# Banded attention: value products on quarters of the array, two shared PSUM banks, and one written order for all engines

## The chip, the cores and the metric

The kernel runs on one core of one Trainium2 chip. The core has five engines with queues of their own: TensorE (PE in the profile; its weight loads are the row PEld), VectorE (DVE), ScalarE (ACT), GpSimd (POOL) and SyncE (SP, which here only issues DMAs). The metric is the device time of one execution in microseconds (us).

## The reference

One step of a two-layer encoder over a prompt of 2048 tokens and a sample of 32 tokens, 1024 channels. The first layer is a gated delta rule, the second a sliding-window attention with learned sinks. Only the second is touched. For a query chunk of 64 tokens it reads the keys and values of its own chunk and of the two before it, so at most 192 keys:

```python
def sink_softmax(s, sinks):
    sk = sinks.astype(jnp.float32)[..., None, None]
    m = jnp.maximum(s.max(-1, keepdims=True), sk)
    p = jnp.exp(s - m)
    return p / (p.sum(-1, keepdims=True) + jnp.exp(sk - m))

def swa_layer(x, k, v, pos, cached, w_in, sinks, w_out, ln_g, ln_b):
    proj = x @ w_in
    q = rope_partial(proj[..., :B_QW].reshape(b, l, B_Q_HEADS, B_HD), pos) * (B_HD ** -0.5)
    z = proj[..., B_QW:]
    o = cached_attention(q, k, v, sk) if cached else banded_attention(q, k, v, sk)
    out = (o * jax.nn.silu(z)) @ w_out
    return layer_norm(DN_ALPHA * x + out, ln_g, ln_b)
```

There are 16 query heads of 64 channels in four groups, one key and value head to a group. The prompt uses the banded form, the sample (32 tokens) a cached window of 128 keys and its own 32. All is float32.

## The kernel before

Up to the attention the kernel projects the input, runs the delta rule and its output layer, and then projects keys, values, queries and the gate z of the second layer in blocks of 416 tokens, in weight slabs of 128 columns (`project`, L74: three f32r products for each of 8 k, high by high, high by low and low by high part). Queries, gates, keys and values go to scratch in HBM (`bq`, `bz`, `bk`, `bv`). The last gate blocks, tokens 0 to 831 of slabs 4 to 7, are computed beside the first chunks; therefore the chunks go in the order 14 to 31, then 0 to 13.

`Attention.chunk(n)` handles 64 queries. It has two passes p, each over two key-value heads (`half` 0 and 1) of four query heads. In a pass:
- scores: four float32 products, each with 64 channels as rows; `half` 0 uses rows 0 to 63, `half` 1 rows 64 to 127 (L1596, out `S`). In the profile a float32 product stands as two passes.
- `softmax` (L1465): largest score (L1470) and minimum with the sink (L1471) on DVE, four exponentials with row sums on ACT (L1478), the sink's exponential (L1479, L1480), sum and reciprocal on DVE (L1481, L1482); then POOL multiplies the probabilities by it (L1604, twice).
- six transposes on PE into two `tr` banks (L1611), copied to `pt` by ACT (L1613) and DVE (L1615).
- values: `vd` holds, for each chunk of 64 keys, a 128 by 128 matrix with the two heads' values on its diagonal and zeros off it. One product for each of up to three key chunks adds up in `ot` (L1617). DVE multiplies by the gate into `graw` (L1620).

After every second chunk a tile of 128 tokens is complete and queued in `pend`. `finish` (L1485) makes its output: high and low part of the gated rows (ACT L1491, POOL L1492), then for each half c of the 1024 output columns 24 products of 512 columns (L1124 to L1126, out `po`), the addition to the residual (L1132), statistics (L1504), a reciprocal root in three Newton steps (L490 to L494), the normalisation on ACT (L1513) and two passes over 1024 columns on POOL (L1514, L1515).

PSUM has eight banks: two scores tiles of two banks, two for transposes, one for values and one for output products. The order of instructions in this stage is not written: a scheduler places them by a modelled timeline. It has PE run products wherever a chunk waits. `flush` keeps two or three finished tiles in reserve for that, and the rest is made after the last chunk, in the scores' banks (`late`).

Of the kernel before, what the change touches and what calls it, by code (L numbers as in the profile page):

```python
# [1069 lines left out]
def load_kept_weights(nc, pool, kept):  # L1070

    w = pool.tile([128, 2, KC, D], F32R, tag="wo", name="wo")
    yield w[:, 0], w[:, 1]
    for k in range(KC):
        nc.sync.dma_start(w[:, :, k].bitcast(F32), kept[:, k].rearrange("a p d -> p a d"))
        yield


# [38 lines left out]
def out_products(nc, ps, ghi, glo, w, k, cs, n):  # L1117

    a, z = k == 0, k == KC - 1
    if n <= 64:  # L1120
        nc.tensor.matmul(ps[:2 * n], ghi[:, k, :2 * n], w[0][:, k, cs], start=a, stop=z, skip_group_check=True)
        nc.tensor.matmul(ps[:n], ghi[:, k, :n], w[1][:, k, cs], start=False, stop=z, skip_group_check=True)
        return
    nc.tensor.matmul(ps[:n], ghi[:, k, :n], w[0][:, k, cs], start=a, stop=False)  # L1124
    nc.tensor.matmul(ps[:n], ghi[:, k, :n], w[1][:, k, cs], start=False, stop=False)  # L1125
    nc.tensor.matmul(ps[:n], glo[:, k, :n], w[0][:, k, cs], start=False, stop=z)  # L1126
# [12 lines left out]
class OutNorm:  # L1139
# [30 lines left out]
    def tile(self, parts, r, n, tail=False):  # L1170
# [5 lines left out]
        for c in range(2):  # L1176
            cs = slice(c * 512, c * 512 + 512)
            ps = self.pp.tile([128, 512], F32, tag="po", name="po")
            for k in range(KC):
                out_products(nc, ps, ghi, glo, w, k, cs, n)  # L1180
                if k % 2 == 1:
                    yield (4 if n <= 64 else 6) * 0.227
# [228 lines left out]
class Attention:  # L1411


    def __init__(self, tc, left, I, O, T, G):
# [4 lines left out]
        self.two = new_pool(tc, left, "t_two", 2, side=L)  # L1419
        self.thr = new_pool(tc, left, "t_thr", 3, side=L)  # L1420
# [6 lines left out]
        self.vd = one.tile([128, 32, 2, 128], F32, tag="vd", name="vd")  # L1427
# [10 lines left out]

    def open_right(self, right):
# [4 lines left out]
        self.pp = new_pool(tc, right, "u_pp", 1, PSUM, side=R)  # L1444
        self.ps_s.append(new_pool(tc, right, "u_ps", 1, PSUM, side=R))
        self.rest = load_kept_weights(self.nc, self.oone, self.T["wob"])
        self.w = next(self.rest)
        next(self.rest)
        self.tabs = ln_tables(self.nc.sync, self.oone, I["b_ln_g"], I["b_ln_b"])

    def load_kv(self, a, z):
        nc, T = self.nc, self.T
        nc.sync.dma_start(self.kT[:, :, a * 64:z * 64], T["bk"][:, :, a * 64:z * 64].rearrange("a p t -> p a t"))
        src = T["bv"][0:NP, :].rearrange("(c k) (p d) -> k c p d", k=64, p=2)
        for i in range(2):
            rows, off = slice(i * 64, i * 64 + 64), slice(64 - i * 64, 128 - i * 64)
            nc.gpsimd.memset(self.vd[rows, a:z, :, off], 0.0)
            for p in range(2):
                nc.sync.dma_start(self.vd[rows, a:z, p, rows], src[:, a:z, p, rows])
# [4 lines left out]

    def softmax(self, S, P, nskc):  # L1465

        nc, V, thr = self.nc, self.nc.vector, self.thr
        nsub = len(P)
        nm = thr.tile([128, 4], F32, tag="nm", name="nm")
        V.tensor_reduce(out=nm[:, :nsub], in_=S, axis=AX.X, op=ALU.max, negate=True)  # L1470
        V.tensor_tensor(out=nm[:, :nsub], in0=nm[:, :nsub], in1=nskc, op=ALU.min)  # L1471
        sm = thr.tile([128, 4], F32, tag="sm", name="sm")
        es_ = thr.tile([128, 4], F32, tag="es", name="es")
        for u in range(nsub):
            src = S[:, u, :]
            if len(P[u].shape) == 3:
                src = src.rearrange("r (j k) -> r j k", k=64)
# [104 lines left out]
    def chunk(self, n):  # L1582
# [38 lines left out]
        if n % 2 == 1:  # L1621
            self.pend.append(((n - 1) * 64, 128, graw))
# [284 lines left out]
```

## Time and profile before

| | us |
|---|---|
| median of 3 runs | 2173.01 (2172.12 to 2175.58) |
| the profiled execution | 2172.59 |
| its span, first to last instruction | 2170.7 |
| PE busy | 2136.9 (98%) |
| DVE, ACT, POOL busy | 1369.1, 898.9, 837.7 |
| first scores pass of the attention (L1596) | 1749.6 |

The attention stage is what comes after about 1730 us. Busy time of PE counts overlapping passes once. Where a line of a timeline has a count (x6), the row merges so many instructions of one kind: its duration is from the first start to the last end. In summaries of one line, three numbers are the shortest, median and longest duration in ns. "[... <-X]" is idle time before an instruction and what ended it.

### The profile page before, as it was taken

The numbers are of one execution on the slowest core, as the hardware profiler recorded it, in microseconds if no ns is written. First come the engines' busy times: TensorE is split into PE (matmuls) and PEld (weight loads), VectorE is DVE, ScalarE is ACT, GpSimd is POOL, SyncE is SP. The second block draws the span as 40 slices with busy tenths as digits, with TensorE's granted clock in tenths as the row PEclk, the third lists the DMA queues.
The fourth block names the chain that finished last, engine by engine and source line by source line (L and its number), as shares of the span: only waits on it lengthen the run. The fifth ranks groups of instructions, "written<-read, shape, count | busy, mean of one in ns | idle before, by whom it ended". The sixth has DMA issues, their size and how long they took to land.

```text
span 2170.7 us, 36895 instructions
## 1 busy us (share of the span) xinstructions
PE 2136.9 (98%) x13690; PEld 1973.4 (91%) x13690; DVE 1369.1 (63%) x2718; ACT 898.9 (41%) x2273; POOL 837.7 (39%) x1185
## 2 busy tenths in 40 slices
PE   8999999999999999999999999999999999999998
PEld 6999999999999999999988888999999987778885
DVE  3676666765648688779868875035442236668775
ACT  4444444356522466667742213221112235444442
POOL 1422222212132377767811102155441215546564
PEclk9999999999999999999999999999999999999999
DMA  5213323257575544447747755364211287233321
GB/s 200 69 60 100 108 91 110 72 163 223 152 229 154 170 162 157 149 161 231 257 146 230 225 174 154 101 233 154 75 69 67 87 193 256 79 98 97 107 64 53
DMA packets 268116, 308.28 MB, mean 142 GB/s; under 512 B 79729, under 2 KB 198833, under 8 KB 267665
## 3 DMA queue, kind: packets, MB, share of 16 engines
q1 hardware_dynamic: 256688, 282.45, 41.7%
q10 hardware_dynamic: 11248, 23.48, 3.3%
q8 instruction: 108, 1.77, 0.3%
q14 instruction: 72, 0.58, 0.1%
HBM read 189.63 MB, written 116.60 MB: 141 GB/s over the span
## 4 chain that ended last, share of the span: by engine, by line
PE 93%; DVE 3%; DMA 2%; ACT 1%; issue 0%; POOL 0%; ACTq 0%; DVEq 0%; POOLq 0%
PE ps L78 17%; PE ps L80 17%; PE ps L79 17%; PE po L1124 5%; PE po L1126 5%; PE po L1125 5%; PE ot L1617 4%; PE S L1596 2%; PE tr L1611 2%; PE g L674 1%; PE ks L816 1%; PE gq L801 1%; PE sp L816 1%; PE op L840 1%; PE vp L816 1%; PE op L846 1%
## 5 line engine op out<-in xcount | busy, mean ns | idle before, releaser
L78 PE MATMUL ps<-act_hi,w_hi 128*128 128x416 f32 x2000 | 706.4, 354 | 3.0 <-ACT w_hi L54 2.3
L80 PE MATMUL ps<-act_hi,w_lo 128*128 128x416 f32 x2000 | 705.0, 353 | 1.3 <-POOL w_lo L55 1.1
L79 PE MATMUL ps<-act_lo,w_hi 128*128 128x416 f32 x2000 | 701.2, 351 | 0.4 <-DVE act_lo L70 0.4
L78 PEld LDWEIGHTS ps<-act_hi,w_hi 128*128 128x128 f32 x2000 | 376.8, 189 | 8.8 <-ACT w_hi L54 3.1
L80 PEld LDWEIGHTS ps<-act_hi,w_lo 128*128 128x128 f32 x2000 | 375.9, 188 | 6.3 <-POOL w_lo L55 1.6
L79 PEld LDWEIGHTS ps<-act_lo,w_hi 128*128 128x128 f32 x2000 | 376.1, 188 | 5.0 <-DVE act_lo L70 0.8
L55 POOL TENSOR_TENSOR w_lo<-w_raw,w_hi 128x1024 fp32r<-128x1024 f32 x44 | 117.0, 2658 | 474.0 <-ACT w_hi L54 437.7
L208 DVE SCALAR_TENSOR_TENSOR y<-R,convw,y 128x2083 f32<-128x2083 f32 x72 | 182.7, 2538 | 62.5 <-ACT y L205 46.8
L1604 POOL TENSOR_TENSOR P<-P,sm 128x384 f32<-128x384 f32 (+2 forms) x128 | 100.5, 807 | 172.0 <-DVE sm L1482 103.6
L708 POOL TENSOR_TENSOR tm<-L,Tt 128x60 f32<-128x60 f32 (+19 forms) x365 | 124.6, 341 | 97.8 <-issue 39.6
L710 POOL TENSOR_TENSOR Tt<-Tt,tm 128x60 f32<-128x60 f32 (+19 forms) x365 | 143.6, 393 | 28.6
L1478 ACT ACTIVATE P<-S,nm 128x192 f32<-128x192 f32 (+3 forms) x260 | 104.8, 419 | 90.2 <-DVE nm L1471 43.6
L304 ACT COPY R<-ps 128x416 f32<-128x416 f32 (+1 forms) x144 | 60.3, 442 | 107.7 <-PE ps L80 96.0
L1124 PE MATMUL po<-wo_hi,g_hi 128*128 128x512 f32 x256 | 103.3, 404 | 0.0
L1322 POOL TENSOR_TENSOR rs<-rs,sin 128x416 f32<-128x416 f32 x50 | 70.7, 1414 | 79.3 <-DVE rs L1321 73.5
L1126 PE MATMUL po<-wo_hi,g_lo 128*128 128x512 f32 x256 | 100.2, 391 | 0.6 <-DVE g_lo L1167 0.6
L1125 PE MATMUL po<-wo_lo,g_hi 128*128 128x512 f32 x256 | 99.9, 390 | 0.0
L1617 PE MATMUL ot<-pt,vd 128*128 128x256 f32 x372 | 97.1, 387 | 1.6 <-ACT pt L1613 1.1
L1407 DVE SCALAR_TENSOR_TENSOR za<-zs,za 128x416 f32<-128x416 f32 x40 | 32.2, 808 | 96.6 <-ACT za L1406 96.5
L1124 PE MATMUL po<-wo,g_hi 128*128 128x512 f32 x224 | 92.9, 415 | 0.0
L54 ACT CAST w_hi<-w_raw 128x1024 fp32r<-128x1024 f32 x48 | 50.4, 1050 | 101.9 <-PE ps L79 74.6
L1126 PE MATMUL po<-wo,g_lo 128*128 128x512 f32 x224 | 90.1, 402 | 0.0
(304 smaller groups left out, 4072.9 us busy)
## 6 DMA issues: line engine op xcount, KB each, us to landing
w_raw<-in_w_in SPq DMA_DIRECT2D x40, 512.0 KB
w_raw<-in_b_w_in SPq DMA_DIRECT2D x20, 512.0 KB
k<-s_k SPq DMA_DIRECT2D x17, 512.0 KB
E<-s_E SPq DMA_DIRECT2D x17, 512.0 KB
s_bz<-za SPq DMA_DIRECT2D x40, 208.0 KB
s_bq<-ra SPq DMA_DIRECT2D x40, 208.0 KB
s_q<-y SPq DMA_DIRECT2D x8, 1024.0 KB
s_wo<-wo_parts SPq DMA_DIRECT2D x16, 512.0 KB
```

The source lines that it names most:

```text
L55: sub.tensor_tensor(out=lo[:], in0=raw[:], in1=hi[:], op=ALU.subtract)
L78: nc.tensor.matmul(ps, hi[:, k, :], xh[:, k, :], start=(k == 0), stop=False)
L79: nc.tensor.matmul(ps, hi[:, k, :], xl[:, k, :], start=False, stop=False)
L80: nc.tensor.matmul(ps, lo[:, k, :], xh[:, k, :], start=False, stop=(k == KC - 1))
L208: nc.vector.scalar_tensor_tensor(out=y[:], in0=R[:, j:j + W], scalar=self.convw[:, i, j:j + 1], in1=y[:], op0=ALU.mult, op1=ALU.add)
L708: P.tensor_tensor(out=tm[:n, i0 - k:, :w], in0=L[:n, i0:, j:j + 1].to_broadcast(sh), in1=Tt[:n, j:j + 1, :w].to_broadcast(sh), op=ALU.mult)
L710: P.tensor_tensor(out=Tt[:n, i0:, :w], in0=Tt[:n, i0:, :w], in1=tm[:n, i0 - k:, :w], op=ALU.subtract)
L1124: nc.tensor.matmul(ps[:n], ghi[:, k, :n], w[0][:, k, cs], start=a, stop=False)
L1125: nc.tensor.matmul(ps[:n], ghi[:, k, :n], w[1][:, k, cs], start=False, stop=False)
L1126: nc.tensor.matmul(ps[:n], glo[:, k, :n], w[0][:, k, cs], start=False, stop=z)
L1478: nc.scalar.activation(P[u], src, AF.Exp, bias=nm[:, u:u + 1], scale=1.0, accum_out=sm[:, u:u + 1])
L1617: nc.tensor.matmul(ot[:, p], self.vd[:, kc0 + j, p, :], pt[:, 2 * j:2 * j + 2, :], start=(j == 0), stop=(j == nj - 1))
```

## The change

Three things change together, all in the second layer's attention.

Values: `vd` is now 64 columns wide and has no zeros. For each key chunk there are four products of 64 rows by 64 columns (p and `half`), each on its own quarter of the array. The rows are the keys of one half, the output partitions p * 64 to p * 64 + 63; the two halves go to two banks. The order of heads in the gate's weight slabs, and that of the rows of the output weights, is changed on the host to match.

Banks: the output products of column half c use the same bank as the values of `half` c (`out_bank`). The bank that held them alone is gone; the scores' banks no longer hold output products.

Order: `chunk`, `softmax` and `finish` are cut into small steps, and `run` writes them out in one order for all five engines, with scores two chunks ahead of the values, transposes one chunk ahead, and the output products of one tile spread over two chunks. `step` places single steps of the previous tile's normalisation between other DVE operations. The gate pieces (12 products each) are placed among the first chunks with `fill`. Slabs 6 and 7, still loaded, go first, so that only slabs 4 and 5 are loaded again. Two of the eight k slices of the output weights are loaded early, into room on the left.

```diff
-        self.vd = one.tile([128, 32, 2, 128], F32, tag="vd", name="vd")
+        self.vd = one.tile([128, 32, 2, 64], F32, tag="vd", name="vd")
...
-            nc.gpsimd.memset(self.vd[rows, a:z, :, off], 0.0)
...
+    def out_bank(self, i):
+        return self.ps_o.tile([128, 512], F32, tag=("oa", "ob")[i], name="ot")
...
+    def product(self, x, c, part):
+        cs = slice(c * 512, c * 512 + 512)
+        if part == 0:
+            x.ps = self.out_bank(c)
+        for k in range(part * KC // 2, (part + 1) * KC // 2):
+            out_products(self.nc, x.ps, x.ghi, x.glo, (self.w[k][:, 0, cs], self.w[k][:, 1, cs]), k, x.n)
...
+    def norm(self, x):
+        nc, V, pool, n = self.nc, self.nc.vector, self.otwo, x.n
+        x.mv = pool.tile([128, 2], F32, tag="mv", name="mv")
+        V.bn_aggr(out=x.mv[:n], in_=x.st[:n])
+        yield
...
+        yield from newton_steps(nc, pool, ve, x.rs, n, 1, "ln")
...
+    def affine(self, x):
+        n, tabs = x.n, self.tabs
+        self.nc.gpsimd.tensor_tensor(out=x.r[:n], in0=x.r[:n], in1=tabs[0][:n], op=ALU.mult)
+        self.nc.gpsimd.tensor_tensor(out=x.r[:n], in0=x.r[:n], in1=tabs[1][:n], op=ALU.add)
...
+    def values(self, n, pts):
+        nc = self.nc
+        kc0, nj = self.keys(n)
+        banks = [self.out_bank(half) for half in range(2)]
+        for j in range(nj):
+            for p in range(2):
+                for half in range(2):
+                    hs, ps = slice(half * 64, half * 64 + 64), slice(p * 64, p * 64 + 64)
+                    nc.tensor.matmul(banks[half][ps, :256], self.vd[hs, kc0 + j, p, :], pts[p][hs, 2 * j:2 * j + 2, :],
+                                     start=(j == 0), stop=(j == nj - 1))
+        return banks
...
+        def largest(i, p, between=iter(())):
+            if i <= last:
+                x = soft[i, p]
+                self.largest(x)
+                step(1)
+                next(between, None)
+                self.with_sink(x)
+
+        def exps(i, p):
+            if i <= last:
+                x = soft[i, p]
+                self.exps(x)
+                step(1)
+                self.sink_exp(x)
+
+        def shares(i, p):
+            if i <= last:
+                x = soft.pop((i, p))
+                self.total(x)
+                step(1)
+                self.inverse(x)
+                self.shares(x)
...
+        fill(3)
+        early(0, 0)
+        fill(2)
+        shares(0, 0)
+        early(0, 1)
+        fill(2)
+        shares(0, 1)
+        early(1, 0)
+        turn(0, 0)
+        copies(0, 0)
+        fill(2)
+        turn(0, 1)
+        copies(0, 1)
+        shares(1, 0)
+        score(1, 1)
+        fill(1)
+        po = following = stored = None
+        for i in range(last):
+            c = i % 2
+            if c == 0:
+                if i >= 4:
+                    done, po = po, following
+                if i + 4 < last and i != 2:
+                    self.start(order[i + 4])
...
+            banks = self.values(order[i], got(i))
+            gated = self.gated(order[i], banks, c)
+            lean = i < 4
+            largest(i + 1, 1, iter(()) if lean else gated)
+            exps(i + 1, 1)
+            drain(gated)
+            if i < 2:
+                fill(1)
+            score(i + 2, 0)
+            turn(i + 1, 0)
+            if lean:
+                largest(i + 2, 0)
+                shares(i + 1, 1)
+                copies(i + 1, 0)
+                exps(i + 2, 0)
+            else:
+                copies(i + 1, 0)
+                largest(i + 2, 0)
+                exps(i + 2, 0)
+            if i < 2:
+                fill(2)
+            if po:
+                self.product(po, c, 0)
+            if i >= 5:
+                x = po if c else done
+                if x:
+                    self.stats(x, 1 - c)
+                    if c == 0:
+                        norm[:] = x, self.norm(x)
+            step(2)
+            if not lean:
+                shares(i + 1, 1)
+            step(4)
+            shares(i + 2, 0)
+            if c == 0 and i >= 2:
+                following = self.finish(*self.pend.pop(0))
+                self.cast(following)
+                self.rest(following)
+            if c == 1 and norm[0]:
+                step(20)
+                self.normed(norm[0])
+                self.affine(norm[0])
+                stored, norm[0] = norm[0], None
+            if c == 0 and stored:
+                self.store(stored)
+                stored = None
+            if po:
+                self.product(po, c, 1)
+                self.added(po, c)
+            turn(i + 1, 1)
+            copies(i + 1, 1)
+            if i == 1:
+                self.start(order[6])
+                opened()
+            score(i + 2, 1)
...
-    for n in order:
-        for _ in range(2):
-            next(att.rest, None)
-        att.chunk(n)
...
+    with tc.manual_schedule(engines={ET.PE, ET.DVE, ET.Activation, ET.Pool, ET.SP}):
+        att.load_keys(12, 18)
+        att.start(14)
+        att.load_values(12, 18)
+        att.start(16)
+        att.run(gates(), opened)
```

Here `cast` and `rest` are the high and low part (ACT, POOL), `normed` is the normalisation on ACT, `added` and `stats` the addition to the residual and the statistics, and `turn`/`turned` the transposes. After the loop `run` makes the tiles that are left (the last two and the sampled one) with the same steps, and the last one ends in `tail` on DVE as before.

More of the change, by code (lines that the diff above doesn't have):

```diff
@@ L2 @@
 import math
+import types
 from contextlib import ExitStack
@@ L1485, in finish, with open_softmax @@
[L1485 to L1494 removed]
+    def open_softmax(self, S, P, nskc, whole):
+        x = types.SimpleNamespace(S=S, P=P, nskc=nskc, whole=whole, n=len(P))
+        x.nm, x.sm, x.es = (self.thr.tile([128, 4], F32, tag=t, name=t)[:, :x.n] for t in ("nm", "sm", "es"))
+        return x
```

470 lines of the change are left out of this document (292 added, 178 removed).

## The prediction

> **What bounds the kernel now.** I read the page first, for the span and for the engine that fills it.
>
> ```profile
> span 2170.7 us, 36895 instructions
> PE 2136.9 (98%) x13690; PEld 1973.4 (91%) x13690; DVE 1369.1 (63%) x2718; ACT 898.9 (41%) x2273; POOL 837.7 (39%) x1185
> ```
>
> The change touches only the attention stage, the last 440 us, so I asked next for a window of its steady part (columns: window, its length, busy time of PE, PEld, DVE, ACT, POOL, granted clock, DMA share, GB/s), and then for the chain of waits there.
>
> ```profile
> 2004.40:2094.00 89.60, 89.60 (x514) 73.19 (x513) 69.01 (x186) 44.89 (x169) 54.69 (x46) 1.00 0.31 90
> ```
>
> ```profile
> 1998.62 1.30 PE ot L1617 x6
> 1999.91 0.55 PE tr L1611 x5
> 2000.95 1.50 PE S L1596 x16
> ```
>
> ```profile
> 2045.77 1.50 PE S L1596 x16
> ```
>
> PE never stops in that window, and the chain runs on PE alone. From one double scores block to the fourth after it are 44.82 us, so one chunk of 64 tokens takes 11.20 us. Of that, 12 value passes at 1.30/6 = 0.217 us are 2.60; 12 transposes at 0.11 are 1.32; 16 score passes are 1.50; the remaining 5.8 us are the 24 output products that go with each chunk, and the changes between them. DVE is second, 69.0 of 89.6 us. Why it is so full shows in the timelines of POOL and DVE of one stretch, and in one line's summary (minimum/median/maximum in ns):
>
> ```profile
> 2046.46 2.35 POOL L1514 TENSOR_TENSOR r<-r,ln_g 128x1024 f32<-128x1024 f32 x1
> 2048.89 2.39 POOL L1515 TENSOR_TENSOR r<-r,ln_b 128x1024 f32<-128x1024 f32 x1
> ```
>
> ```profile
> 2045.81 0.69 DVE L1132 SCALAR_TENSOR_TENSOR r<-r,po 128x512 f32<-128x512 f32 x1
> 2046.53 0.69 DVE L1504 BATCH_NORM_STATS2 st<-r 128x6 f32<-128x512 f32 x1
> 2047.14 0.94 DVE L1470 TENSOR_REDUCE nm<-S 128x4 f32<-128x768 f32 x1
> 2048.11 0.72 DVE L1471 TENSOR_TENSOR nm<-nm,nsk 128x4 f32<-128x4 f32 x1
> 2048.75 0.94 DVE L1470 TENSOR_REDUCE nm<-S 128x4 f32<-128x768 f32 x1
> 2049.62 1.68 DVE L1479 TENSOR_TENSOR es<-nm,nsk 128x4 f32<-128x4 f32 x1
> 2051.23 0.15 DVE L1471 TENSOR_TENSOR nm<-nm,nsk 128x4 f32<-128x4 f32 x1
> 2051.41 0.16 DVE L1479 TENSOR_TENSOR es<-nm,nsk 128x4 f32<-128x4 f32 x1
> 2051.49 0.42 DVE L1620 TENSOR_TENSOR graw<-ot,zs 128x256 f32<-128x256 f32 x1
> 2051.82 0.15 DVE L1481 TENSOR_TENSOR sm<-sm,es 128x4 f32<-128x4 f32 x1
> 2051.89 0.55 DVE L1615 COPY pt<-tr 128x384 f32<-128x384 f32 x1
> ```
>
> ```profile
> L1479 DVE TENSOR_TENSOR es<-nm,nsk x64: 107/162/2352, 1751.7 to 2127.2; 128x4 f32<-128x4 f32 x64
> ```
>
> A four-column subtraction takes 0.16 us, but 1.68 at 2049.62, and it ends at 2051.30, just as POOL's 2.39 us pass (to 2051.28) ends; the one at 2048.11 ends with the POOL pass before. The longest of the 64 is 2.35, one POOL pass. A DVE operation with two small SBUF inputs waits out the POOL pass that is running, and DVE's queue waits behind it; the reduce, the copy and the gating product, each with an input in PSUM, pass freely (the reduce at 2047.14 ran inside a POOL pass). Today this costs little, since PE has products to run meanwhile. Starts also show that independent operations follow each other about 0.08 us before the end of the last, dependent ones 0.03 after.
>
> **PE work of one chunk after the change.** Scores come as two separate blocks, with the values between them.
>
> ```profile
> 1850.07 0.40 PE L1124 MATMUL po<-wo,g_hi 128*128 128x512 f32 x1
> 1850.39 0.92 PE L1596 MATMUL S<-kT,qs 64*128 64x192 f32 x8
> 1851.24 0.55 PE L1611 MATMUL tr<-ident,P 128*128 128x128 f32 x3
> ```
>
> A lone scores block holds PE for 0.85 us (1850.39 to 1851.24), and entering it costs 0.1 more (0.32 after the product, against 0.23 between products): two cost 1.9, against 1.50. The same 0.2 us is my price for entering the values in their own shape. Eight score passes on two halves of the rows in 0.85 us show already that halves run together. For quarters the trace has this pair, on one quarter and then on two that share neither rows nor columns:
>
> ```profile
> 746.33 1.08 PE L753 MATMUL tp<-y,u 64*64 64x64 f32 x15
> ```
>
> ```profile
> 747.31 1.10 PE L763 MATMUL up<-u,y 64*64 64x64 f32 x31
> ```
>
> Twice as many passes in the same time. Nothing in the trace has two column halves on the same rows. Per key chunk the new code issues eight quarter passes: if all four quarters overlap they fill two slots of 0.217, so 6 slots or 1.30 us for a chunk; if only the row halves overlap, 2.60 as now. I take 1.30, nearest to the L763 row, where quarters overlap fully. The page "TensorE: Matmul & The Clock Gate" of the Trainium skill (Part 3, packing) gives 2.38 times for three column tiles, not 3; read so, two would give about 1.6, and the values 1.6 us (an estimate from that page), which in the twenty or so chunks that PE sets would make the sum 6 us longer. Sum for PE: 1.30 + 0.2 + 1.9 + 1.32 + 5.6 (24 x 0.233) = 10.3 us a chunk, 0.9 less than now.
>
> **What the written order makes of it.** Every engine is now in fixed order, so I walked one pair of chunks through it, time 0 being the first value pass. Three more prices:
>
> ```profile
> L1478 ACT ACTIVATE P<-S,nm 128x192 f32<-128x192 f32 x240 | 98.0, 424 | 86.7 <-DVE nm L1471 40.7 <-DVE ve L1508 16.9 <-PE ot L1617 15.8
> ```
>
> ```profile
> L1604 POOL TENSOR_TENSOR P<-P,sm 128x384 f32<-128x384 f32 x120 | 96.6, 827 | 161.9 <-DVE sm L1482 101.8 <-DVE ln_t L490 18.2 <-DVE es L1479 16.1
> ```
>
> ```profile
> L1492 POOL TENSOR_TENSOR g_lo<-graw,g_hi 128x1024 fp32r<-128x1024 f32 x16 | 38.5, 2409 | 11.1 <-ACT g_hi L1491 10.4 <-PE S L1596 0.6
> ```
>
> Odd chunk (`affine` is queued at its end). POOL is still in `rest` of the even one until 2.9. The Newton step that DVE has ahead of the first gating is a two-input operation, so it waits to 2.9; from there step, gating, minimum, gating, copy (0.47), reduce and minimum (0.97), statistics (0.6), sum and reciprocal take 4.0, to 6.9. POOL multiplies the shares of (i+1, 1) from 7.05 to 8.65, those of (i+2, 0) to 10.2, and then runs `affine`, two passes of 2.4, to 15.0. PE needs the first shares only at the end of its products, which begin 0.4 late and end at 9.0; transposes, scores and the copies bring the next values at 10.7.
>
> Even chunk. `affine` therefore lasts to 15.0 - 10.7 = 4.3. `with_sink` or at the latest `sink_exp`, both two-input, comes at about 2.0 and sticks behind it; behind them wait gating, copy, reduce and statistics. From 4.3: 0.2 for the two small ones, gating 0.34, copy 0.47, reduce and its minimum 1.15, `stats` 0.7, mean and variance 0.3, sum and reciprocal 0.4, hand-over 0.2: shares start on POOL 3.7 us later, at 8.0, and end at 9.7. PE's products ended at 8.6; it idles 1.1 us. Two Newton steps stick behind the two POOL passes, then sum, reciprocal, `added` (0.6) and the copy (0.47) follow: next values at 4.3 + 7.35 = 11.65. The second shares run from 10.5 to 12.1 and `rest` to 14.55, which is 2.9 into the odd chunk, where I began.
>
> The shared banks add two waits: a half tile's products wait for the gating that empties their bank (the half they need is gated first, at 2.0 or 3.3, when PE is at 3.0), and the next values wait for `added`, which lies in the walk. On SP the store of the rows waits for `affine`; the loads behind it are four chunks ahead of their use, so that costs nothing.
>
> So a pair takes 10.7 + 11.65 = 22.35 us, against 22.4 now: what PE saves, the DVE-POOL loop takes back. The cover of the softmax's small operations, free PE work in any order, is gone.
>
> **The stage as a sum.** The start and the end:
>
> ```profile
> 1730.40 0.52 ACT L1405 ACTIVATE zs<-ps 128x416 f32<-128x416 f32 x1 [3.61 <-PE ps L80]
> ```
>
> ```profile
> 1733.62 1.97 SPq L1433 DMA_DIRECT2D sks<-in_sinks_s  x4
> ```
>
> ```profile
> 1738.01 0.43 SPq L1453 DMA_DIRECT2D kT<-s_bk  x1
> ```
>
> ```profile
> 1741.94 1.16 SPq L1577 DMA_DIRECT2D qs<-s_bq  x2
> ```
>
> ```profile
> 1740.00:1745.00 5.00, 5.00 (x28) 4.95 (x28) 0.64 (x2) 1.32 (x3) 0.00 (x0) 1.00 0.99 231
> ```
>
> ```profile
> 1800.00:1805.00 5.00, 3.44 (x21) 2.40 (x23) 3.44 (x11) 4.06 (x20) 1.17 (x3) 1.00 1.03 414
> ```
>
> ```profile
> 2160.16 0.40 PE L1126 MATMUL S<-wo,g_lo 128*128 128x512 f32 x1
> ```
>
> ```profile
> 2167.75 0.34 ACTq L1523 DMA_DIRECT2D out_y<-r  x1
> ```
>
> The three-block gates end at 1730.3. SP sends the sinks until 1735.6, then keys and queries, 1.6 us of issue and 0.9 MB at 231 GB/s (4 us): the first scores at 1741.5, while the three gate pieces ahead of them end at 1737 (36 matmuls at 0.19), so PE idles 4 us. Four score blocks (3.8), two transposes (1.4) and seven gate pieces of 2.27 bring the first values at 1762.6. Chunks 0 and 1 have three gate pieces and no products: 4.7 + 6.8 and about 0.5 for the single scores tile, 12 each, to 1786.6. Chunks 2 and 3 have nothing beside them; the loop scores, reduce, exponentials (1.7), sum, shares (1.6), transposes gives 7.5 and 7.7, to 1801.8. The six late weight slices, 6 MB asked for at 1786, take 15 us at 414 GB/s and just arrive. Chunks 4 to 7, before the first `affine` falls on an even chunk: 10.3 x 3 + 10.7, to 1843.3. Twelve pairs, 268.2, less 1.5 for the two short chunks: 2110. Then four half tiles of products (22.4), the sampled one (32 x 0.23 = 7.4), 0.8 of sampled values and 1.5 of waits: 2142. Last product to end as now, 10.5. Span 2152.7.
>
> The execution profiled took 2172.59 with this span of 2170.7, 1.9 outside; the median of the runs, 2173.01, is 0.4 above. Forecast: 2152.7 + 1.9 + 0.4 = 2155 us. Since the pairs give nothing, the 18 us come from the start (up to chunk 7) and the end of the stage, and a slip there goes straight into the sum. Edits at nothing: the zero fills of `vd` and two of four weight splits go, on POOL, ACT and DVE, beside PE's gates; if they were not covered they could only give a gain of under 3 us.
>
> **The rivals.** First, column halves do not overlap. For: no row shows them. Against: the quarters of L763. Values stay 2.60, a chunk without POOL waits costs 11.6; odd 11.6 and even 11.6 make a pair of 23.2. Twelve times 0.85 and eight times 1.3: 2155 + 20 = 2175, and the change doesn't do what its name says.
>
> Second, the lock costs a whole further pass in each pair, and the time ends above today's: `normed` sits behind the exponentials on ACT, and if it comes so late that both passes of `affine` fall into the even chunk, its end moves from 4.3 to 6.7. Twelve times 2.4: 2184. It decides once a pair exceeds 23.85, that is 1.5 us (18/12) over mine. For: the 0.16 us operations measured at 2.35. Against: in my walk `normed` ends at 8.8 and POOL is free for it at 10.2.
>
> Third, DVE slips between POOL's passes and PE sets the pace: pairs of 20.6, 12 x 1.75 = 21 less, 2134. Against: the two rows above that stuck. The page "SBUF — State Buffer" of the Trainium skill (Who interferes with whom) says that a two-input DVE instruction blocks fully while GpSimd reads; this trace agrees (1.68 us), and by it this rival needs POOL idle.
>
> Fourth, late data: keys or weights 10 to 15 us later in the unhidden start (DMA at 0.99 there), 2168.
>
> **How the numbers follow.** Forecast 0.44 (its own range 2145 to 2166), third 0.2, second 0.18, first 0.11, fourth 0.07. The range 2130 to 2188 takes in all but the tails. 0.2% is 4.3 us, about what a measurement here can tell: faster is the forecast, the third, and a little of the others, 0.66; same, most of the first and part of the fourth, 0.12; slower 0.22.
>
> **What would show it.** Value passes starting four at a time, 1.3 us a chunk (right), or two at a time (first rival). Pairs of 22 to 23 us with PE idle about 1 us ahead of the transposes of even chunks, ended by POOL's shares, and two-input DVE operations of over 2 us early in even chunks. Even chunks as long as odd ones at 10.3 would prove the loop wrong; a first value pass after 1768 would prove the start wrong.

## The result and the profile after

The changed kernel takes 2166.79 us (median of 13 runs, 2165.36 to 2170.42) against 2172.78 (13 runs, 2170.57 to 2175.58) for the kernel before, run beside it: ratio 0.9975, 95% interval 0.9966 to 0.9983. It is faster, by 6 us where 18 were forecast. The profiled execution is the longest of the 13, 2170.42 us.

The page of the kernel after: the span, and the busy time of each engine.

```profile
span 2168.6 us, 37497 instructions
PE 2112.2 (97%) x14062; PEld 1936.5 (89%) x14062; DVE 1385.8 (64%) x2717; ACT 892.3 (41%) x2271; POOL 825.6 (38%) x1179
```

PE is busy 24.7 us less than before (2136.9), but the span is only 2.1 shorter: PE stands idle 22.6 us more. Some of the span is the run itself: the gate block that was copied at 1730.40 before, with nothing of the change ahead of it, is copied at 1734.27 here (first row of the timeline of ACT below), so this execution was 3.9 us late when the attention began.

The values' work, as a group of instructions (here and in the before row: busy us, mean ns of one):

```profile
L1701 PE MATMUL ot<-pt,vd 64*64 64x256 f32 x744 | 51.4, 403 | 7.2 <-DVE r L1125 7.2
```

```profile
L1617 PE MATMUL ot<-pt,vd 128*128 128x256 f32 x372 | 97.1, 387 | 1.6 <-ACT pt L1613 1.1 <-DVE pt L1615 0.5
```

Twice the passes in half the time: the four quarters run at once. In the trace the four passes of a set start 6 to 7 ns apart, and the sets 0.22 us apart. Next, the timelines of PE, DVE and POOL over one steady pair of chunks (start, us; the bracket is idle time and what ended it).

```profile
2040.10 1.53 PE L1701 MATMUL ot<-pt,vd 64*64 64x256 f32 x24
...
2049.78 0.76 PE L1683 MATMUL tr<-ident,P 128*128 128x128 f32 x5 [0.46 <-POOL P L1504]
...
2051.33 1.53 PE L1701 MATMUL ot<-pt,vd 64*64 64x256 f32 x24
...
2061.82 0.45 PE L1701 MATMUL ot<-pt,vd 64*64 64x256 f32 x4
```

```profile
2042.01 2.34 DVE L1483 TENSOR_TENSOR nm<-nm,nsk 128x4 f32<-128x4 f32 x1
...
2048.25 0.71 DVE L493 TENSOR_TENSOR ln_t<-ln_t,ln_y 128x1 f32<-128x1 f32 x1
```

```profile
2041.97 2.37 POOL L1559 TENSOR_TENSOR r<-r,ln_b 128x1024 f32<-128x1024 f32 x1
2048.12 1.61 POOL L1504 TENSOR_TENSOR P<-P,sm 128x384 f32<-128x384 f32 x2 [3.78 <-DVE ln_y L487]
```

The even chunk takes 11.23 us, the odd one 10.49: 21.72 a pair, against 22.4 before. The four-column minimum of the even chunk stands 2.34 us and ends, at 2044.35, with POOL's bias pass (2044.34). POOL starts on the shares 8.0 us into the chunk, and PE waits for them (0.46 us at 2049.78).

The loss lies at the start of the stage. The same 105 us as windows (length, PE, PEld, DVE, ACT, POOL, granted clock, DMA share, GB/s), after and before:

```profile
1745.00:1850.00 105.00, 84.77 (x572) 67.51 (x574) 46.07 (x114) 43.22 (x167) 28.74 (x32) 0.90 0.84 228
```

```profile
1745.00:1850.00 105.00, 97.36 (x555) 79.33 (x554) 59.69 (x153) 51.31 (x198) 39.59 (x40) 0.98 0.79 224
```

PE idles 20.2 us there, 12.6 more than before, and its clock is lower. Two waits make most of it. The first, in the timelines of ACT, DVE and PE and in a window:

```profile
1734.27 0.52 ACT L1398 ACTIVATE zs<-ps 128x416 f32<-128x416 f32 x1 [3.60 <-PE ps L81]
...
1738.81 0.52 ACT L1398 ACTIVATE zs<-ps 128x416 f32<-128x416 f32 x1 [3.61 <-PE ps L81]
...
1759.10 1.04 ACT L55 CAST w_hi<-w_raw 128x1024 fp32r<-128x1024 f32 x1 [7.24 <-DMA w_raw<-in_b_w_in]
1762.82 0.42 ACT L1490 ACTIVATE P<-S,nm 128x192 f32<-128x192 f32 x1 [2.68 <-DVE nm L1483]
```

```profile
1760.17 1.23 DVE L56 TENSOR_TENSOR w_lo<-w_raw,w_hi 128x1024 fp32r<-128x1024 f32 x1 [7.69 <-ACT w_hi L55]
```

```profile
1747.03 0.92 PE L1660 MATMUL S<-kT,qs 64*128 64x192 f32 x8 [1.45 <-DMA qs<-s_bq]
...
1764.59 1.65 PE L1660 MATMUL S<-kT,qs 64*128 64x192 f32 x8 [6.29 <-ACT P L1490]
...
1768.55 0.55 PE L79 MATMUL ps<-act_hi,w_hi 128*128 128x416 f32 x1
...
1770.50 0.36 PE L79 MATMUL ps<-act_hi,w_hi 128*128 128x416 f32 x1
...
1777.39 1.53 PE L1701 MATMUL ot<-pt,vd 64*64 64x256 f32 x24
```

```profile
1765.00:1775.00 10.00, 10.00 (x53) 8.97 (x51) 5.57 (x11) 4.96 (x16) 1.61 (x2) 0.73 1.21 254
```

ACT has a weight slab to cast that has not landed. Behind it in ACT's queue stand the exponentials of the second score block. DVE stands too: it waits for the cast with the slab's low part (L56), and the second block's largest scores, which the exponentials need, come behind that. The third score block needs the bank of the second. When PE starts again, a gate pass takes 0.55 us instead of 0.36, up to 1770.3: the clock is halved for 5.7 us (granted 0.73 over the window shown, 0.50 from 1765.0 to 1770.3), which costs 2.8 more (half of the 5.7, an estimate). The second wait, on SP, DVE and PE:

```profile
1813.88 16.38 SPq L1464 DMA_DIRECT2D vd<-s_bv  x4
1830.35 0.96 SPq L1511 DMA_DIRECT2D r<-s_h  x1
```

```profile
1836.52 0.69 DVE L1125 SCALAR_TENSOR_TENSOR r<-r,ot 128x512 f32<-128x512 f32 x1 [9.44 <-DMA r<-s_h]
```

```profile
1837.26 2.84 PE L1701 MATMUL ot<-pt,vd 64*64 64x256 f32 x24 [7.24 <-DVE r L1125]
```

SP stands 16.4 us in the issue of four value loads; the residual rows come behind them. The addition that empties the shared bank waits for those rows, and the sixth chunk's values wait for the bank. The values then take 2.84 us instead of 1.53, the clock being low again (0.58 granted from 1837 to 1843).

### The profile page after: what moved, and what is told of

Read it like the earlier page. It is cut to its first block, busy times and chain, and to the rows that moved or that the text cites. A ratio compares the mean times of both kernels' runs of the same rounds, so it can differ in the third digit from the quotient of the medians.

```text
span 2168.6 us, 37497 instructions
## 1 busy us (share of the span) xinstructions
PE 2112.2 (97%) x14062; PEld 1936.5 (89%) x14062; DVE 1385.8 (64%) x2717; ACT 892.3 (41%) x2271; POOL 825.6 (38%) x1179
## 4 chain that ended last, share of the span: by engine, by line
PE 86%; DVE 6%; DMA 3%; SPq 2%; ACT 1%; POOL 1%; issue 1%; ACTq 0%; POOLq 0%; DVEq 0%
PE ps L79 17%; PE ps L81 17%; PE ps L80 17%; PE po L1119 3%; PE po L1117 3%; PE po L1118 3%; PE ot L1117 2%; PE ot L1701 2%; PE ot L1119 2%; PE ot L1118 2%; PE S L1660 2%; PE tr L1683 1%; PE ks L817 1%; PE gq L802 1%; PE g L675 1%; DVE nm L1483 1%
## 5 line engine op out<-in xcount | busy, mean ns | idle before, releaser
L56 POOL TENSOR_TENSOR w_lo<-w_raw,w_hi 128x1024 fp32r<-128x1024 f32 x44 | 117.1, 2661 | 473.8 <-ACT w_hi L55 437.8
L1504 POOL TENSOR_TENSOR P<-P,sm 128x384 f32<-128x384 f32 (+3 forms) x130 | 101.5, 805 | 214.1 <-DVE sm L1500 117.8
L1490 ACT ACTIVATE P<-S,nm 128x192 f32<-128x192 f32 (+2 forms) x260 | 105.1, 425 | 147.0 <-DVE nm L1483 97.5
L1117 PE MATMUL ot<-wo,g_hi 128*128 128x512 f32 x256 | 103.9, 406 | 1.5 <-DVE graw L1712 1.3
L1119 PE MATMUL ot<-wo,g_lo 128*128 128x512 f32 x256 | 101.1, 395 | 0.0
L1118 PE MATMUL ot<-wo,g_hi 128*128 128x512 f32 x256 | 101.1, 395 | 0.0
```

The lines of the kernel that those rows point to most:

```text
L56: sub.tensor_tensor(out=lo[:], in0=raw[:], in1=hi[:], op=ALU.subtract)
L1117: nc.tensor.matmul(ps[:n], ghi[:, k, :n], hi, start=a, stop=False)
L1118: nc.tensor.matmul(ps[:n], ghi[:, k, :n], lo, start=False, stop=False)
L1119: nc.tensor.matmul(ps[:n], glo[:, k, :n], hi, start=False, stop=z)
L1490: self.nc.scalar.activation(x.P[u], src, AF.Exp, bias=x.nm[:, u:u + 1], scale=1.0, accum_out=x.sm[:, u:u + 1])
L1504: self.nc.gpsimd.tensor_tensor(out=P, in0=P, in1=f, op=ALU.mult)
```

## The experiments

My theory was: the forecast was missed through these two waits, and what is left in the steady part is the DVE-POOL loop. The rivals are in the expectations. Ratios are to the kernel before on the same chip, with 95% intervals; the kernel as changed has 0.9975.

**The slab.** `late_split` moves the cast and its low part one gate piece back, behind the exponentials:

```
-                if b == 0:
+                if b == 1:
                     if j in (1, 2):
                         p2.w[3 + j] = split_fetched(nc, p2.wp, raw, nc.vector)
-                    if j < 2:
+                    if j == 1:
+                        raw = fetch_weights(nc, p2.wp, I["b_w_in"][12 + j])
+                else:
+                    if j == 0:
...
```

The second slab's fetch, which needs the freed buffer, goes with it.

> The two late weight slabs of the gates are split one gate piece later, behind the softmax of the second score block instead of ahead of it. Theory A (the start of the stage lost its time because the exponentials stood on ACT behind a weight slab that had not landed): PE's 6.3 us of idleness before the third score block goes, and the slow clock after it too (some 2.8 us); the first value pass comes some 9 us earlier against the gate pieces, and the kernel takes some 2158 us, 0.994 of the kernel before. Rival B (keys, queries and value rows are late anyway, the slab only happened to be the last of them): the idle time stays, with another cause, and the kernel takes 2165 to 2167.

Measured 2161.99 us, 0.9943 (0.9931 to 0.9956). Timelines of ACT and PE:

```profile
1752.65 0.42 ACT L1490 ACTIVATE P<-S,nm 128x192 f32<-128x192 f32 x1 [2.98 <-DVE nm L1483]
...
1757.38 1.05 ACT L55 CAST w_hi<-w_raw 128x1024 fp32r<-128x1024 f32 x1 [2.11 <-DMA w_raw<-in_b_w_in]
```

```profile
1756.03 0.92 PE L1660 MATMUL S<-kT,qs 64*128 64x192 f32 x8
```

The third score block runs at 1756.03 with no idle time of note, and from the first scores to the first values there are 22.3 us instead of 30.4. The cast still waits for its data, but behind the exponentials. Part of the gain is lost again: the second slab's cast now waits 2.92 us for its data in the first chunk, with its low part and PE's gate passes behind it, and that chunk takes 14.56 us instead of 12.29. 0.32% or 7 us: theory A, a little under its size.

**The rows.** `late_keys` takes `load_keys(0, 12)` and `load_values(0, 12)` out of `opened` and calls them at chunk 8.

> The keys and values of the first twelve chunks, which are not used before the sixteenth chunk of the order, are fetched at the eighth one instead of together with the late output weights. Theory A (the first residual rows came late because SP stood 16 us in the issue of those value fetches): the rows' fetch is issued some 16 us earlier, PE's 7.2 us before the sixth chunk's values go, with the slow clock behind them some 9 us in all, and the kernel takes some 2158 us, 0.994. Rival B (the rows wait for the 6 MB of weights, whose transfer is in front of them in any case): the idle time shrinks by less than 3 us, 2164 to 2167.

Measured 2159.33 us, 0.9931 (0.9918 to 0.9945), 0.44% or 9.5 us: theory A. Timelines of SP and PE:

```profile
1807.48 1.03 SPq L1511 DMA_DIRECT2D r<-s_h  x1
1808.87 10.46 SPq L1642 DMA_DIRECT2D qs<-s_bq  x2
```

```profile
1814.16 2.35 PE L1701 MATMUL ot<-pt,vd 64*64 64x256 f32 x24
1825.21 1.53 PE L1701 MATMUL ot<-pt,vd 64*64 64x256 f32 x24
```

Counted from the first values, the rows are issued 18 us earlier, and the fifth chunk takes 11.05 us instead of 19.11. SP still stands 10.46 us in an issue, but now of loads that nobody waits for yet.

> Both edits of the loads together. Theory A: the two losses lie one behind the other, so both gains add, some 18 us, to about 2149 us, 0.989 of the kernel before; PE idles less than 6 us between the start of the stage and the eighth chunk. Rival B (the second is only a shadow of the first: what is gained at the start is waited for at the output weights): the sum is no more than the better of the two alone, 2156 to 2160.

Measured 2152.73 us, 0.9901 (0.9888 to 0.9915), 16 us under the changed kernel by the ratios: the two add (7 and 9.5). PE still idles 9.5 us between the start of the stage and the eighth chunk, where I expected under 6. This version is the base of all that follows but `row_pairs`.

**The quarters.** `row_pairs` puts the loop over `p` outermost in `values`, on the kernel as changed.

> The same 24 value passes of a chunk, in another order: first all of one pair of column halves, then all of the other, so that only two quarters, on different rows, can run together. Theory A (four quarters run at once, and in the written order a chunk of tokens is set by PE in the odd ones and by the loop of DVE and POOL in the even ones): the values take 2.6 us a chunk instead of 1.3 to 1.5, odd chunks become some 1.2 us longer, even ones less than that, and with the chunks of the start the kernel takes 25 to 35 us more, 2190 to 2200. Rival B (the quarters gave nothing, and the written order alone made what was gained): the values take as long as before, and the kernel 2165 to 2168.

Measured 2169.00 us, 0.9977 (0.9968 to 0.9986). The timeline of PE:

```profile
2038.32 2.01 PE L1701 MATMUL ot<-pt,vd 64*64 64x256 f32 x24
...
2049.39 2.01 PE L1701 MATMUL ot<-pt,vd 64*64 64x256 f32 x24
...
2060.09 2.01 PE L1701 MATMUL ot<-pt,vd 64*64 64x256 f32 x24
```

Neither reading fits: my edit did not do what I had said. The values take 2.01 us and not 2.6, since passes of the second pair of quarters start while the first is still at work: by the starts in the trace, 0.50 us after the first pass, when three of the first pair's six turns are still to come. The half microsecond it does cost goes into PE's slack: the pair is 21.77 instead of 21.72. So the run could not tell whether PE's time counts, and I went back to full blocks. `full_blocks` has `vd` with its zeros, 12 full passes, a bank for each `p`, and gate and output weights laid out as before the change; `quarters_same_room` has its smaller buffers with quarters.

> On top of both load edits, the values are taken back to full blocks: 12 passes over the whole array, half of each block zeros, two quarters' worth of work in each. The blocks need more room, so one early weight slice, one buffer of the gated rows and one of the softmax go; the next run has quarters with the same room. Theory A (PE's time counts in the written order once its slack is used up, as the two-by-two order suggests, where 0.5 us more in each chunk made a pair only 0.06 longer): 1.2 to 1.3 us more for PE in each chunk is more than the slack of about 1 us in a pair, so pairs go from 21.7 to some 23, and the kernel takes 15 to 25 us more than the next run. Rival B (the loop of DVE and POOL alone sets the chunks): pairs stay within 0.3 us of 21.7, and the kernel within 6 us of the next run.

> Both load edits, quarters, and the smaller room of the run before it (one early weight slice instead of two, two buffers for the gated rows, three for the softmax). Theory A: the buffers taken away were not waited for and the seventh late slice lies 2 to 3 us behind in the transfers, so pairs stay at 21.7 and the kernel takes 2152 to 2157. Rival B: the third and fourth buffers carried the order, and pairs grow by over 0.5 us, to over 2158.

Measured 2173.89 us, 1.0001 (0.9993 to 1.0010), against 2153.15, 0.9906 (0.9891 to 0.9921). Full blocks, the timeline of PE and a window:

```profile
2027.04 2.86 PE L1700 MATMUL ot<-pt,vd 128*128 128x256 f32 x12
...
2038.59 2.86 PE L1700 MATMUL ot<-pt,vd 128*128 128x256 f32 x12
```

```profile
2000.00:2080.00 80.00, 80.00 (x446) 63.78 (x445) 59.72 (x162) 37.27 (x144) 45.65 (x38) 1.00 0.32 87
```

With full blocks PE never stops, and every chunk takes 11.55 us, a pair 23.1. The quarters are worth 20.7 us here. Without them the written order, even with both loads mended, is no faster than the kernel before.

**The loop.** `no_bias_pass` leaves out one POOL line of `affine`, the addition of the layer norm's bias.

> On top of both load edits, the second of the two POOL passes of the layer norm's end (adding its bias) is left out except for the last tile, so that POOL is free 2.4 us earlier in each pair. Theory A (the POOL pass that reaches into the even chunk sets its length through the waiting minimum): the minimum no longer waits over 2 us in even chunks, they take 10.5 instead of 11.2, and the kernel takes about 2143. Rival B (even chunks are 11.2 for another reason): pairs within 0.2 us of 21.7 and 2150 to 2154.

Measured 2135.82 us, 0.9829 (0.9816 to 0.9843), 16 us less than `both_loads` by the ratios, where I expected 10. One line's summary (ns, minimum/median/maximum) and the timeline of PE:

```profile
L1483 DVE TENSOR_TENSOR nm<-nm,nsk x45: 145/154/165, 1854.0 to 2075.6; 128x4 f32<-128x4 f32 x45
```

```profile
2022.56 1.53 PE L1700 MATMUL ot<-pt,vd 64*64 64x256 f32 x24
...
2032.78 1.53 PE L1700 MATMUL ot<-pt,vd 64*64 64x256 f32 x24
...
2043.00 1.53 PE L1700 MATMUL ot<-pt,vd 64*64 64x256 f32 x24
```

No minimum waits any more, and both kinds of chunk take 10.22: the odd ones too had been longer than PE's own work. That leaves open whether POOL's work or DVE's wait for it was the cause. So `psum_both` keeps POOL's work and changes DVE's operands:

```
-        self.nc.vector.tensor_reduce(out=x.nm, in_=x.S, axis=AX.X, op=ALU.max, negate=True)
+        self.nc.vector.tensor_reduce(out=x.raw, in_=x.S, axis=AX.X, op=ALU.max, negate=True)
...
-        self.nc.vector.tensor_tensor(out=x.nm, in0=x.nm, in1=x.nskc, op=ALU.min)
+        self.nc.vector.tensor_tensor(out=x.nm, in0=x.raw, in1=x.nskc, op=ALU.min)
...
-        self.nc.vector.tensor_tensor(out=x.es, in0=x.nm, in1=x.nskc, op=ALU.subtract)
-        self.nc.scalar.activation(x.es, x.es, AF.Exp)
+        self.nc.vector.tensor_tensor(out=x.es, in0=x.raw, in1=x.nskc, op=ALU.subtract)
+        self.nc.vector.tensor_scalar(out=x.es, in0=x.es, scalar1=0.0, scalar2=None, op0=ALU.min)
+        self.nc.scalar.activation(x.ex, x.es, AF.Exp)
```

Here `x.raw` and `x.ex` are spare columns of the scores tile `S`, in PSUM, and `total` adds `x.ex`.

> On top of both load edits, the softmax's small DVE operations read one operand from PSUM: the negated maximum and the sink's exponential go into spare columns of the scores tile, so that the minimum, the sink's difference and the sum have one small SBUF input each instead of two (one single-input minimum is added; the Newton steps stay as they are). Theory A (an operation with two small SBUF inputs waits out the POOL pass, and this is what makes even chunks longer than odd ones): none of the three takes over 0.3 us any more, even chunks go from 11.2 to about 10.5, and the kernel takes about 2143, 9 to 10 us less than with the load edits alone. Rival B (the Newton steps, still with two SBUF inputs, take over the wait, or PE's own work is 11.2 in even chunks): pairs stay at 21.5 to 21.8, and the kernel at 2150 to 2154.

Measured 2253.34 us, 1.0369 (1.0355 to 1.0383), a miss on both sides. The summary of the difference's line shows where it goes:

```profile
L1495 DVE TENSOR_TENSOR es<-S,nsk x47: 160/163/164, 1857.6 to 2192.4; 128x4 f32<-128x4 f32 x47
...
its engine sat idle before it (us, times) until:
  ACT P L1492: 85.5, 48
```

Reading the tile behind the exponentials, DVE waits for ACT, 1.8 us each time. `psum_early` takes the difference right behind the minimum.

> Both load edits and the small operands in PSUM as before, but the sink's difference is taken right behind the minimum, ahead of the exponentials, so that DVE doesn't wait for ACT there (in the run with the difference behind them that wait took 1.8 us, 48 times). Theory A (the minimum that waits out the POOL pass sets the even chunks): the stall of the minimum is gone without a new wait, even chunks go from 11.2 to 10.3 or 10.5, and the kernel takes 2139 to 2144 instead of 2152.7. Rival B (the exponential that ends in the scores tile, or the tile's later release, brings a new wait): pairs over 21.7 and the kernel at 2153 or more.

Measured 2153.49 us, 0.9910 (0.9896 to 0.9923): no gain, pairs of 21.72. Timelines of DVE and POOL:

```profile
1959.43 0.15 DVE L1485 TENSOR_TENSOR nm<-S,nsk 128x4 f32<-128x4 f32 x1
1959.50 0.15 DVE L1486 TENSOR_TENSOR es<-S,nsk 128x4 f32<-128x4 f32 x1
1959.69 1.96 DVE L1496 TENSOR_SCALAR es<-es 128x4 f32<-128x4 f32 x1
```

```profile
1959.24 2.37 POOL L1562 TENSOR_TENSOR r<-r,ln_b 128x1024 f32<-128x1024 f32 x1
```

These are the case's clearest rows. The minimum and the difference, each with an operand in PSUM, start inside POOL's pass and are through in 0.15 us; the next operation, one input and one output in SBUF, stands until that pass ends (1961.61). In most pairs it stands longer, up to 2.25 us. The wait was not tied to two inputs, as I had written, and it moved by one instruction. Nor does every operation in SBUF wait: in the kernel after, the reciprocal (L1500, four columns, SBUF to SBUF) started inside a POOL operation 12 times and took 0.18 us each time. `psum_all` puts that operation's data into PSUM too (`x.es` becomes columns of `S`), `psum_all_bias4` adds the moved bias pass told of further down.

> As the version with the sink's difference taken early, but the difference stays in the scores tile, so that the single-input minimum behind it, which stood 2.23 us inside a POOL pass there, reads and writes PSUM. Theory A (any small DVE operation whose operands all lie in SBUF waits out the POOL pass, with one input as with two, and this wait is what makes even chunks 11.2): nothing of the softmax's first half waits any more, even chunks go to 10.3 to 10.5 and the kernel takes 2139 to 2145. Rival B (the next SBUF operation, the variance's or the sum's, takes the wait over, or PE is at its end): pairs of 21.5 to 21.7 and 2150 to 2154.

> The same together with the bias pass moved and cut into four. Theory A: the two remove different waits (the first half of the softmax; the even chunk as a whole), PE's 10.22 sets every chunk, and the kernel takes 2135 to 2138. Rival B (the Newton steps and the sums, still in SBUF, are the last to wait in either): no better than the four quarters alone, 2139 to 2142.

Measured 2241.20 us, 1.0328 (1.0313 to 1.0342), and 2239.80, 1.0313 (1.0298 to 1.0328): again outside both readings. I had left the operation behind the exponentials, and there it waits 1.8 us for ACT, 49 times. `psum_first` takes it ahead of them, next to the difference.

> The same as the version with all of the small operands in PSUM, but with the single-input minimum taken ahead of the exponentials too: there DVE waited 1.8 us for ACT's reads of the same tile, 49 times, which was the whole of that version's loss. Theory A (small DVE operations with all operands in SBUF wait out the POOL pass, and this sets the even chunks): with neither wait, even chunks take 10.3 to 10.5 and the kernel 2139 to 2145 against 2152.7 with the load edits alone. Rival B (the wait moves on to the next operation in SBUF, or the shares come late for another reason): pairs 21.5 to 21.7, the kernel 2150 to 2154.

Measured 2138.31 us, 0.9842 (0.9828 to 0.9855). The two lines' summaries and the timeline of PE:

```profile
L1485 DVE TENSOR_TENSOR nm<-S,nsk x45: 144/152/164, 1854.8 to 2076.5; 128x4 f32<-128x4 f32 x45
```

```profile
L1487 DVE TENSOR_SCALAR S<-S x47: 168/170/171, 1855.1 to 2086.3; 128x4 f32<-128x4 f32 x45, 128x2 f32<-128x2 f32 x2
```

```profile
2023.48 1.53 PE L1704 MATMUL ot<-pt,vd 64*64 64x256 f32 x24
2033.70 1.53 PE L1704 MATMUL ot<-pt,vd 64*64 64x256 f32 x24
```

All of POOL's work is there, no small operation of the softmax's first half waits, and every steady chunk is 10.22. That part of theory A is shown: the wait set the chunks, not POOL's load. Its wording, that any small operation in SBUF waits, is too wide, as the reciprocal shows. The Newton steps, still in SBUF, stand 1.4 us in most pairs (1.64 at the longest) where nobody waits for them.

**Moving the pass instead.** `bias_in_2` and `bias_in_4` leave the operands and run the bias pass one chunk later, behind `rest`, in two or four pieces; `bias2_psum` and `psum_first_bias4` add the PSUM operands.

> Both load edits; the bias pass of POOL is moved behind the next low part of the gated rows, some 12 us later, where POOL idles in the odd chunk, in two halves of 512 columns; the store follows it. Nothing is left out. Theory A (it is the place of the POOL pass, not its work, that costs; leaving it out made every chunk 10.22): even chunks 10.2, the minimum of odd chunks waits some 1 us for a half, so a pair takes 20.5 to 21.0 and the kernel 2136 to 2143. Rival B (DVE sticks in the odd chunk as it did in the even one): pairs 21.4 to 21.9, the kernel 2149 to 2155.

> The same with the bias pass in four quarters. Theory A (a waiting DVE operation gets its turn between two POOL instructions, so that shorter ones cost it less): pairs as long as with two halves or up to 0.3 us shorter, 2134 to 2142. Rival B (the instructions' own overhead on POOL, some 0.2 us each, eats that): 2 to 5 us above the version with halves.

> Both load edits, the moved bias pass in halves and the small operands in PSUM. Theory A (PE's own work is 10.22 us a chunk, and with no stall left on DVE it sets every chunk): pairs of 20.4 to 20.5 and the kernel at 2135 to 2138. Rival B (each of the two removes the same stall, or the Newton steps hold what is left): no more than 1 us better than the better one of the two alone.

> That version with the bias pass moved and cut into four. Theory A: the waits that the one and the other remove are the last ones, every chunk takes PE's 10.22, and the kernel 2135 to 2138. Rival B (with the pass moved there is no wait of the softmax left to remove): 2139 to 2142, as with the four quarters alone.

Two pieces: 2150.75 us, 0.9895 (0.9882 to 0.9909), rival B; four: 2140.20, 0.9847 (0.9833 to 0.9860), the time of theory A, but with pairs 1.1 us shorter than with two pieces where at most 0.3 were expected. The timelines of DVE and POOL with two:

```profile
2032.19 0.98 DVE L1483 TENSOR_TENSOR nm<-nm,nsk 128x4 f32<-128x4 f32 x1
2033.10 1.32 DVE L495 SCALAR_TENSOR_TENSOR ln_y<-ln_t,ln_y 128x1 f32<-128x1 f32 x1
```

```profile
2031.88 2.53 POOL L1564 TENSOR_TENSOR r<-r,ln_b 128x512 f32<-128x512 f32 x2
```

DVE gets one operation through at the end of each piece, so a long piece is a long wait: the pair is 21.6, and 20.5 with four pieces. `bias2_psum`, built on the operands of `psum_early`, took 2141.65 us, 0.9853 (0.9840 to 0.9866), neither reading: better than halves alone by 9, and some chunks still 11.5. `psum_first_bias4` took 2138.09 us, 0.9843 (0.9830 to 0.9857), the same as `psum_first`: its steady chunks are 10.22 too, PE's own work, so moving the pass adds nothing there. `psum_first`, with the pass where it was, is the version to keep: by the ratios 34 us faster than the kernel before, 29 faster than the change alone.

## Why the prediction was right and wrong

**PE's work, right.** Four quarters at once, 24 passes in six slots; 10.3 us a chunk forecast, 10.22 measured where nothing else holds PE. The first rival (no overlap of column halves, chunks of 11.6) describes `full_blocks` (11.55), not the change.

**The loop, right in kind, 3% too long.** `affine` was to end 4.3 us into the even chunk (4.24 measured; the second rival needed 6.7), the shares to start at 8.0 (8.0), PE to wait for them (1.1 us forecast, 0.6 measured). The two Newton steps stuck behind the shares until 9.64, against 9.7 in my walk. Too long were the ends of both chunks: from there to the next values I took 1.95 and 1.59 were measured, and the odd chunk, which I had at 10.7, takes 10.49. So a pair is 21.72, not 22.35, and 12 of them were worth 7.6 us more than forecast. The four chunks with and around the two short ones took 3.6 us less than two steady pairs where I took 1.5. The rule "two small SBUF inputs" was too narrow. The page "SBUF — State Buffer" of the Trainium skill (Who interferes with whom) has `tensor_scalar` among the operations that can contend with GpSimd, and excepts those with at most one SBUF input outside certain modes; the 1.96 us row and the 0.15 us rows of `psum_early` agree with both halves of this.

**The start, wrong.** The failing step is the sum up to chunk 7. "Chunks 4 to 7 ... to 1843.3" came out at 1870.14, or 1866.2 without the 3.9 us, 22.9 too late. In order:
- "The three-block gates end at 1730.3": the row that I quoted is of the last block but one, and the last is copied at 1738.81 here (1734.9). That is 4.6 us, most of which come back, because PE then waits 1.45 for the queries instead of 4; the first scores are 1.6 late.
- "Four score blocks, two transposes and seven gate pieces bring the first values at 1762.6": 1777.39, or 1773.5. I counted PE's work and no queue. Of the weight splits the two that stay were not priced, only the two that go. 9.3 us from first scores to first values, 6.3 of them the wait for the slab and 2.8 the slow clock behind it. The text's own mark, first values after 1768, is passed.
- "The six late weight slices just arrive": they do. But of what SP holds behind them I priced nothing, though `finish` issues the rows' load there, and I wrote of SP that its loads are four chunks ahead. It cost 8.8 us in chunk 4, and 2.2 in the chunk after, whose values run at the low clock. Chunks 0 to 3 are 1.6 over in all, chunks 6 and 7 together 0.6 under.

The fourth rival (late data at the start, 2168), with a chance of 0.07, is nearest to what happened. It was sized as one delay of 10 to 15 us of keys or weights; there were two, a cast that stood waiting for its weights ahead of the softmax and a residual load issued behind big ones, and they and the rest of the start cost 22.9. That its 2168 is close to the measured 2167 is luck. The third rival (PE sets the pace, 20.6 a pair) holds only with the lock removed (20.44). The tail was 0.7 over: 11.2 us from the start of the last product to the end, 10.5 forecast.

The sum, in this execution less its 3.9 us: 22.9 late at chunk 8 and 12.0 late at the end, so 10.9 came back in between. Of these 7.6 are the pairs and 2.1 the short chunks; where the other 1.2 come from stays open. 2155 + 12 is the measured median. That the miss is no larger is luck too: two errors of opposite sign.

## What to carry to other kernels

When an order is written by hand, walk each queue, not only the busiest engine: a load that is small and needed soon must be issued ahead of big ones, and a cast that waits for data must not stand ahead of work on the critical path. A small operation of DVE in SBUF can cost a whole POOL pass (2.35 us here); one operand in PSUM took the minimum out of that, but the operation behind it must be looked at too, and any new reader of a shared tile. An edit that shortens PE's work is worth only what the slowest loop lets through: here half of the quarters' 1.33 us a chunk until that loop was mended.

## What was not expected of the hardware

- PE ran at a lower clock after both idle times of 6 to 7 us: half for 5.7 us after the first (0.50 granted from 1765.0 to 1770.3). The clock added 30 to 45% to what each wait cost (2.8 on 6.3 and 2.2 on 7.2, estimates). The page "TensorE: Matmul & The Clock Gate" of the Trainium skill (Part 1) has the clock halved after an idle window of about 3.4 us; these two waits agree. Shorter gaps did it too: after idle times of 1.74 and 0.45 us, 0.33 apart, the fifth chunk's values (1818.15) also took 2.84 us, with 0.81 granted from 1815 to 1820. How little idle time is enough, no run here settles.
- SP's issue of four value loads, 0.75 us each in the stage's first ones, took 16.4 us behind 7 MB of weights and tables, and held back everything else that SP had to issue. I read this as a full queue that holds the issuing engine; the trace shows only the long issues.
- In `row_pairs`, passes of free quarters started ahead of the end of the ones before them, so that the order in pairs cost 0.5 us instead of 1.3.
- Why DVE waited for ACT on the shared scores tile in three of the kernels (1.8 us, 48 or 49 times) stays open: the trace shows the wait, not whether the chip or only the order of the program asks for it.
